# Second mixer of a two-layer encoder on one Trainium2 core: the fourth gated projection is written ahead of the attention

## The chip, the core and the metric

One core of a Trainium2 chip computes the whole network in one launch. Its engines are TensorE (PE, matrix products; PEld is its weight loading), VectorE (DVE), ScalarE (ACT, activation functions from tables that have to be loaded), GpSimd (POOL) and SyncE (SP, which issues DMAs). Each engine works through its own list of instructions in a fixed order; semaphores tie the lists together. The metric is the device time of one execution in microseconds (us), lower is better.

## The reference, cut to what matters

Two sequences of 256 tokens (512 tokens in all, width 1024, fp32) go through two layers. Layer 0 is another mixer and a feed-forward block; layer 1 is the mixer below and a feed-forward block of the same kind. The change touches only layer 1's mixer.

```
def odd_mixer(x, ...):
    h = x @ w_in
    c_q, c_kv, k_r, glu_a, glu_g = jnp.split(h, [o1, o2, o3, o4], axis=-1)
    c = latent_attention(c_q, c_kv, k_r, ...)          # 8 heads, softmax over 256 keys
    d = glu_a * jax.nn.sigmoid(glu_g)                  # 512 channels
    d = jax.nn.silu(layernorm(dwconv(d, conv_w, conv_b), conv_ln_g, conv_ln_b))   # 31 taps
    return jnp.concatenate([c, d], axis=-1) @ w_out
```

## The kernel before, in words

Every fp32 matrix product is split into three products of a rounded part and a remainder (`hi`, `lo`); `gemm_feat` issues them (recorded at L95, as all products). The layers run one after the other. A scheduler of the framework turns the written order into one list per engine; it moves instructions by its own estimate of when they can run, so the written order is a preference and not the final order.

In the second mixer the 512 gated channels are handled in four chunks of 128. For chunk i, `glu(i)` computes two products of 24 matrix instructions each, `glu` (value) and `glu` (gate), and calls `gate(i, ...)` at high priority: the sigmoid of the gate into `sig` (ACT, L551), the product into the padded tile `dpad` (DVE, L554), tap 0 of the convolution into `cacc` (DVE, L557), and tap 21 into `acc` (ACT, L559). The other 29 taps of a chunk are split: 20 run on DVE (L719, adding into `cacc`); for 9, ACT multiplies `dpad` by the tap into one of two slots of `pr` (L723) and POOL adds the slot to `acc` (L724). So an ACT product waits until POOL's add of two products earlier is done. L725 joins `cacc` and `acc`; `conv_ln` transposes the result (`ct`, L735), normalizes it and applies SiLU.

`attend(p)` does one pair of heads: per sequence and head a score set `s` (PE), the row maximum `nmx` (DVE, L491), the exponential into `er` with its sum (ACT, L494), the reciprocal `ri` (DVE, L497), the scaling of `er` (ACT, L501; DVE for the last pair), four transposes `pt` (PE, L508), a copy to `PTr` (ACT, L510), and per sequence the product `pv`, which is split into `mixT` (ACT L115, DVE L116). That makes 16 score sets. Only two score banks exist, so the scores of set n+2 wait for the exponential of set n.

Sigmoid and exponential stand in different ACT tables; a switch is an ACT_TABLE_LOAD. `preload(func, src)` runs a one-element activation into `tab` so that a load happens there. After the attention comes the output projection (`op`, `dn` tiles), whose weights and products also fill PE between the attention's last steps, and then the second feed-forward block, matrix products back to back.

Of the kernel before, what the change touches and what calls it, by code (L numbers as in the profile page):

```python
# [49 lines left out]
def tile_encoder(ctx: ExitStack, tc: tile.TileContext, I, O):  # L50
# [17 lines left out]
    def act(shape, dt=F32, s="a"):  # L68
        return actp.tile(shape, dt, tag="act", name=nm(s))

    def tmp(shape, dt=F32, s="t"):
        return tp.tile(shape, dt, tag="tmp", name=nm(s))
# [16 lines left out]
    def bank(pool, s="ps"):  # L89
        return pool.tile([P, 512], F32, tag="b", name=nm(s))  # L90
# [3 lines left out]
    def mm(out, lhsT, rhs, first, last):  # L94
        last_mm[0] = nc.tensor.matmul(out=out, lhsT=lhsT, rhs=rhs, start=first, stop=last)  # L95
# [6 lines left out]
    def preload(func, src):  # L102
        nc.scalar.activation(out=small(1, "tab"), in_=src, func=func)
# [27 lines left out]
    def pc(name, i):  # L131
        o, _ = PCOL[name]
        return par[:, o + i:o + i + 1]

    def gemm_feat(ps, hi, lo, xT, seqs=(0, 1), n=KC):
        if len(seqs) == 2:
            tsl = slice(0, T)
        else:
            tsl = slice(seqs[0] * S, seqs[0] * S + S)
        for k in range(n):  # L140
            xh, xl = xT[k][:, 0, tsl], xT[k][:, 1, tsl]
            wh, wl = hi[:, k * P:(k + 1) * P], lo[:, k * P:(k + 1) * P]
            mm(ps[:, tsl], wh, xh, k == 0, False)
            mm(ps[:, tsl], wh, xl, False, False)
            mm(ps[:, tsl], wl, xh, False, k == n - 1)
# [383 lines left out]
    def glu_load(i, keep=False):  # L529
        return [wload(I["wglu"][:, i, j].rearrange("p k n -> p (k n)"), 1024, keep) for j in range(2)]  # L530

    def odd_mixer(xT):
# [3 lines left out]
        def glu(i, by_seq=False):  # L536
            pss = []
            for hi, lo in kept.pop(i, None) or glu_load(i):
                pss.append((bank(pA, "glu"), hi, lo))
            for seqs in ((0,), (1,)) if by_seq else ((0, 1),):  # L540
                for ps, hi, lo in pss:
                    gemm_feat(ps, hi, lo, xT, seqs)
            with tc.high_priority():
                gate(i, pss[0][0], pss[1][0])

        def gate(i, pa, pg):
            sg = tmp([P, 512], s="sig")
            d = dpad[i]
            out, va = d[:, :, 15:15 + S], pa.rearrange("p (s t) -> p s t", s=2)
            vs = sg.rearrange("p (s t) -> p s t", s=2)  # L550
            nc.scalar.activation(out=sg, in_=pg, func=AF.Sigmoid)  # L551
            if i >= 2:
                preload(AF.Exp, sg[:, 0:1])
            nc.vector.tensor_tensor(out=out, in0=va, in1=vs, op=ALU.mult)  # L554
            accps[i] = bank(pA, "cacc")
            a, a2 = accps[i].rearrange("p (s t) -> p s t", s=2), acc2[i // 2][:, i % 2]
            nc.vector.tensor_scalar(out=a, in0=d[:, :, 0:S], scalar1=pc("cw", i * 32),  # L557
                                    scalar2=pc("cw", i * 32 + 31), op0=ALU.mult, op1=ALU.add)
            nc.scalar.activation(out=a2, in_=d[:, :, 31 - NPOOL:31 - NPOOL + S], func=AF.Copy,  # L559
                                 scale=pc("cw", i * 32 + 31 - NPOOL))  # L560
# [76 lines left out]
        def qproj():  # L637
            cT = G["cT"]
            wq = G["wq"]
            ropeT = G["kr"][:, 1:2, 0:S].broadcast_to([P, 2, S])  # L640
            qT = G["qT"] = [act([P, 2, T], s="qT") for _ in range(4)]

            def qfeat(pool, c):
                ps = bank(pool, "q")
                for k in range(2):
                    wh, wl = wq[k][0][:, c * P:(c + 1) * P], wq[k][1][:, c * P:(c + 1) * P]
                    mm(ps, wh, cT[k][:, 0, :], k == 0, False)
                    mm(ps, wh, cT[k][:, 1, :], False, False)
                    mm(ps, wl, cT[k][:, 0, :], False, k == 1)
                return ps  # L650
            for p in range(4):
                ps = qfeat(pB, 4 + p)
                for h in (0, 1):
                    rows = slice(64 - 64 * h, 128 - 64 * h)
                    nc.vector.tensor_tensor(out=qT[p][rows, h, :].rearrange("p (s t) -> p s t", s=2),  # L655
                                            in0=ps[rows].rearrange("p (s t) -> p s t", s=2), in1=ropeT[rows],
                                            op=ALU.mult)
                ps = qfeat(pC, p)
                for h in (0, 1):
                    rows = slice(64 * h, 64 * h + 64)  # L660
                    nc.scalar.activation(out=qT[p][rows, h, :], in_=ps[rows], func=AF.Copy, scale=96 ** -0.5)
# [20 lines left out]
        def attend(p):  # L682
            if p == 0:
                G["ring"] = Ring(2, "er"), Ring(2, "PTr")
            er, PTr = G["ring"]
            qT, kT = G["qT"][p], G["kT"][p]

            def score(out, qs, ks):
                for h in range(2):
                    mm(out[h], qT[:, h, qs], kT[:, h, ks], True, True)  # L690
            mixT[p] = act([P, 2, T], F32R, "mixT")
            if p == 2:
                G["sink"] = ToFeat(xscr[1], 1, last_mm[0], "ln1_g1", "ln1_b1", xscr[2], ())
            attention(p, score, G["V"], mixT[p], lambda ps, h, e: ps, er, PTr, p < 3, p == 3)
# [7 lines left out]
        kvproj()  # L702
        qproj()
        glu(2)
        attend(0)
        attend(1)
        glu(3)
        op = OutProj("wout1", mixT, [0, 1, 2, 3], [4, 5, 6, 7])
        attend(2)
        op.open(0)  # L710
# [126 lines left out]
    xT = even_mixer()  # L837
    xT = ffn(0, xT, lambda m: ToFeat(xscr[0], 0, m, "ln2_g0", "ln2_b0", xscr[1])).xT
    xT = odd_mixer(xT)
    ffn(1, xT, lambda m: ToOut(xscr[2], 2, m, 3, O["y"]))  # L840

# [80 lines left out]
```

## Time and profile before

| | before |
|---|---|
| time, median of 3 runs (lowest to highest) | 1106.43 us (1104.14 to 1106.67) |
| the profiled execution: its own time | 1104.76 us |
| the profiled execution: span from first to last instruction | 1102.9 us |
| PE busy in the span | 1082.3 us |
| granted TensorE clock, mean over the span | 0.992 |
| window 641.30 to 647.50 us: PE busy | 0.00 us |
| window 680.00 to 780.00 us: PE busy | 99.98 us |

The profile is of one execution, whose own time is 1.86 us longer than its span and 1.67 us shorter than the median of the three timed runs. All times in the trace are counted from the start of the span. PE is nearly always busy; the rows of the places where it is not are what has to be read.

### The profile page before, as it was taken

How to read it: one execution, taken by the hardware profiler on the slowest of the kernel's cores; microseconds unless marked ns; L12 is line 12 of the kernel's file. 1: busy time of each engine (PE TensorE's matmuls, PEld its weight loads, DVE VectorE, ACT ScalarE, POOL GpSimd, SP SyncE). 2: the span in 40 equal slices, each digit the busy share in tenths (PEclk: the TensorE clock that was granted, in tenths of full speed). 3: DMA queues.
4: the chain of work that ended last, by engine and by line, in shares of the span. 5: the costliest groups of instructions: out<-in, count | busy, mean ns of one | idle time of the engine just before them, and what ended most of it. 6: DMA issues, size and time to landing. Idle time of an engine off the chain costs nothing.

```text
span 1102.9 us, 13655 instructions
## 1 busy us (share of the span) xinstructions
PE 1082.3 (98%) x5210; PEld 900.8 (82%) x5210; DVE 673.2 (61%) x996; ACT 488.7 (44%) x783; POOL 226.6 (21%) x222
## 2 busy tenths in 40 slices
PE   9999999999999999999999979999999999999996
PEld 7888778988888888888898856899888888888885
DVE  5378955766565656422578999587665656542227
ACT  5436644544444444421266797355444444431110
POOL 0482001200000000005464661830000000000173
PEclk9999999999999999999999979999999999999999
DMA  7852223533333323645232104254333333222602
GB/s 256 244 141 77 60 103 107 163 105 96 96 96 96 96 96 99 206 166 180 80 122 58 38 20 153 66 172 122 100 96 96 96 96 96 96 96 96 215 34 76
DMA packets 36098, 124.21 MB, mean 113 GB/s; under 512 B 4289, under 2 KB 5057, under 8 KB 36033
## 3 DMA queue, kind: packets, MB, share of 16 engines
q1 hardware_dynamic: 28864, 100.05, 29.5%
q0 software_dynamic: 6448, 22.53, 6.0%
q8 instruction: 41, 0.67, 0.3%
q10 hardware_dynamic: 720, 0.75, 0.2%
q14 instruction: 25, 0.20, 0.1%
HBM read 113.88 MB, written 8.39 MB: 111 GB/s over the span
## 4 chain that ended last, share of the span: by engine, by line
PE 93%; DVE 3%; ACT 2%; issue 1%; DMA 0%; POOL 0%; POOLq 0%; DVEq 0%; ACTq 0%
PE up L95 44%; PE dn L95 29%; PE qk L95 4%; PE op L95 4%; PE glu L95 3%; PE v L95 2%; PE u L95 2%; PE s L95 1%; PE pv L95 1%; PE pt L508 1%; DVE cacc L719 1%; PE lnT L237 1%; DVE wlo L111 1%; DVE qT L655 0%; ACT er L494 0%
## 5 line engine op out<-in xcount | busy, mean ns | idle before, releaser
L95 PE MATMUL up<-xT,whi 128*128 128x512 f32 (+1 forms) x1536 | 439.9, 371 | 0.0
L111 DVE TENSOR_TENSOR wlo<-raw,whi 128x1024 fp32r<-128x1024 f32 (+1 forms) x174 | 238.8, 1374 | 297.4 <-ACT whi L109 296.1
L95 PEld LDWEIGHTS up<-xT,whi 128*128 128x128 f32 x1536 | 279.9, 188 | 49.9
L109 ACT CAST whi<-raw 128x1024 fp32r<-128x1024 f32 (+1 forms) x174 | 182.4, 1050 | 249.1 <-PE dn L95 132.6
L95 PE MATMUL up<-xT,wlo 128*128 128x512 f32 (+1 forms) x768 | 284.0, 372 | 0.0
L95 PE MATMUL dn<-whi,gT 128*128 128x512 f32 x704 | 217.4, 389 | 0.0
L95 PEld LDWEIGHTS up<-xT,wlo 128*128 128x128 f32 x768 | 144.4, 188 | 24.9
L95 PEld LDWEIGHTS dn<-whi,gT 128*128 128x128 f32 x704 | 132.0, 188 | 27.2
L95 PE MATMUL dn<-wlo,gT 128*128 128x512 f32 x352 | 136.9, 389 | 0.0
L186 POOL DMA_DIRECT2D xres<-xscr x12 | 6.5, 546 | 576.0 <-PE dn L95 576.0
L95 PEld LDWEIGHTS dn<-wlo,gT 128*128 128x128 f32 x352 | 66.1, 188 | 13.8
L115 ACT CAST gT<-cv 128x512 fp32r<-128x512 f32 x44 | 27.3, 620 | 111.6 <-DVE cv L782 111.6
L771 ACT ACTIVATE cv<-up,par 128x512 f32<-128x512 f32 x88 | 68.3, 776 | 0.0
L774 DVE SCALAR_TENSOR_TENSOR cv<-up,par,cv 128x510 f32<-128x510 f32 x88 | 65.8, 748 | 2.7
L781 ACT ACTIVATE cv<-cv 128x512 f32<-128x512 f32 x44 | 27.8, 632 | 85.2 <-DVE cv L774 85.2
L772 DVE SCALAR_TENSOR_TENSOR cv<-up,par,cv 128x510 f32<-128x510 f32 x88 | 65.4, 743 | 0.0
L719 DVE SCALAR_TENSOR_TENSOR cacc<-dpad,par,cacc 128x512 f32<-128x512 f32 x80 | 58.9, 750 | 1.1
L724 POOL TENSOR_TENSOR acc<-acc,pr 128x512 f32<-128x512 f32 x36 | 48.7, 1353 | 38.9 <-ACT pr L723 32.2
L116 DVE TENSOR_TENSOR gT<-cv,gT 128x512 fp32r<-128x512 f32 x44 | 30.4, 692 | 27.5 <-ACT gT L115 27.5
L95 PE MATMUL op<-whi,mixT 128*128 128x512 f32 x128 | 44.3, 402 | 0.0
L95 PE MATMUL dn<-whi,mixT 128*128 128x512 f32 x128 | 42.8, 394 | 0.0
L95 PE MATMUL glu<-xT,khi 128*128 128x512 f32 (+1 forms) x160 | 42.0, 349 | 0.0
(195 smaller groups left out, 1351.4 us busy)
## 6 DMA issues: line engine op xcount, KB each, us to landing
raw<-in_wup SPq DMA_DIRECT2D x88, 512.0 KB, 3.6
raw<-in_wdn SPq DMA_DIRECT2D x44, 512.0 KB, 3.5
raw<-in_wout SPq DMA_DIRECT2D x16, 512.0 KB, 3.7
xscr<-xres POOLq DMA_DIRECT2D x12, 512.0 KB, 3.7
xres<-xscr POOLq DMA_DIRECT2D x12, 512.0 KB, 4.4
raw<-in_wqk SPq DMA_DIRECT2D x8, 512.0 KB, 6.6
raw<-in_wglu SPq DMA_DIRECT2D x8, 512.0 KB, 3.8
raw<-in_wug SPq DMA_DIRECT2D x7, 512.0 KB, 3.6
```

Source lines behind the costliest of these rows:

```text
L95: last_mm[0] = nc.tensor.matmul(out=out, lhsT=lhsT, rhs=rhs, start=first, stop=last)
L109: nc.scalar.copy(out=hi[:, :n], in_=raw[:, :n])
L111: nc.vector.tensor_tensor(out=lo[:, :n], in0=raw[:, :n], in1=hi[:, :n].bitcast(F32), op=ALU.subtract)
L115: nc.scalar.copy(out=dst[:, 0, sl], in_=src)
L116: nc.vector.tensor_tensor(out=dst[:, 1, sl], in0=src, in1=dst[:, 0, sl].bitcast(F32), op=ALU.subtract)
L237: nc.tensor.transpose(self.banks[k // 2][:, (k % 2) * S + q * P:(k % 2) * S + q * P + P], x[:, k * P:(k + 1) * P], ident)
L719: nc.vector.scalar_tensor_tensor(out=a, in0=dpad[i][:, :, j:j + S], scalar=pc("cw", i * 32 + j), in1=a, op0=ALU.mult, op1=ALU.add)
L724: nc.gpsimd.tensor_tensor(out=a2, in0=a2, in1=pr, op=ALU.add)
L771: nc.scalar.activation(out=c, in_=pv, func=AF.Identity, scale=pc(fw, ch * 4 + 1), bias=pc(fw, ch * 4 + 3))
L772: nc.vector.scalar_tensor_tensor(out=c[:, :, 1:S], in0=pv[:, :, 0:S - 1], scalar=pc(fw, ch * 4), in1=c[:, :, 1:S], op0=ALU.mult, op1=ALU.add)
L774: nc.vector.scalar_tensor_tensor(out=c[:, :, 0:S - 1], in0=pv[:, :, 1:S], scalar=pc(fw, ch * 4 + 2), in1=c[:, :, 0:S - 1], op0=ALU.mult, o ...
L781: nc.scalar.activation(out=cg, in_=cg, func=AF.Silu)
```

## The change

`glu(3)` is written ahead of `attend(0)` and `attend(1)` in place of behind them, and the load of the exponential's table is asked for once, behind the fourth sigmoid, in place of behind the third and again behind the fourth.

```
             nc.scalar.activation(out=sg, in_=pg, func=AF.Sigmoid)
-            if i >= 2:
+            if i == 3:
                 preload(AF.Exp, sg[:, 0:1])
             nc.vector.tensor_tensor(out=out, in0=va, in1=vs, op=ALU.mult)
...
         kvproj()
         qproj()
         glu(2)
+        glu(3)
         attend(0)
         attend(1)
-        glu(3)
         op = OutProj("wout1", mixT, [0, 1, 2, 3], [4, 5, 6, 7])
```

Since a scheduler sets the lists, the lists themselves show what moves. On ACT, before, this stands from the scaling of the first score set to the exponential of the third (`er_5018` is first used by score sets 0 and 1, `er_5019` by 2 and 3; `sig_5243` is the fourth gate):

```order
L501 ACTIVATE er_5018<-er_5018,ri_5038 128x256 x2
L723 ACTIVATE pr_4428<-dpad_4418,par 128x512
L494 ACTIVATE er_5018,rs_5050<-s_5028,nmx_5048 128x256 x2
L501 ACTIVATE er_5018<-er_5018,ri_5053 128x256 x2
L551 ACT_TABLE_LOAD
L551 ACTIVATE sig_5243<-glu_5194 128x512
L510 COPY PTr_5022<-pt_5042 128x512
L559 ACTIVATE acc_705_4425<-dpad_4421,par 128x512
L723 ACTIVATE pr_4428<-dpad_4421,par 128x512 x2
L494 ACT_TABLE_LOAD
L494 ACTIVATE er_5019,rs_5071<-s_5063,nmx_5069 128x256 x2
```

In the changed kernel ACT has this from the last products of the third chunk to the exponential of the second score set (`sig_5066` is the fourth gate, `er_5074` serves score sets 0 and 1):

```order
L723 ACTIVATE pr_4428<-dpad_4418,par 128x512 x6
L551 ACTIVATE sig_5066<-glu_5017 128x512
L103 ACT_TABLE_LOAD
L103 ACTIVATE tab_5068<-sig_5066 128x1
L559 ACTIVATE acc_705_4425<-dpad_4421,par 128x512
L723 ACTIVATE pr_4428<-dpad_4421,par 128x512 x2
L494 ACTIVATE er_5074,rs_5091<-s_5083,nmx_5089 128x256 x2
L723 ACTIVATE pr_4428<-dpad_4421,par 128x512 x2
L501 ACTIVATE er_5074<-er_5074,ri_5094 128x256 x2
L494 ACTIVATE er_5074,rs_5106<-s_5084,nmx_5104 128x256 x2
```

The two exponentials that stood ahead of the fourth sigmoid now stand behind it, all nine products of the third chunk stand ahead of it, and one table load is left where there were two (a third, behind the third sigmoid `sig_5010`, is gone as well).

On PE, before, the first two score sets stand among the products of the fourth chunk (`glu_5193` value, `glu_5194` gate):

```order
L95 MATMUL glu_5193<-xT_4287,khi_3989 128x512 x2
L95 MATMUL s_5027<-kT_4684,qT_4884 128x256 x2
L95 MATMUL glu_5193<-xT_4287,klo_3991 128x512
L95 MATMUL glu_5194<-xT_4252,khi_3995 128x512 x2
L95 MATMUL glu_5194<-xT_4252,klo_3997 128x512
L95 MATMUL s_5028<-kT_4684,qT_4884 128x256 x2
```

In the changed kernel the 48 products come first and the score sets behind them:

```order
L95 MATMUL glu_5017<-xT_4287,khi_3995 128x512 x2
L95 MATMUL glu_5017<-xT_4287,klo_3997 128x512
L95 MATMUL s_5083<-kT_4684,qT_4884 128x256
L95 MATMUL s_5084<-kT_4684,qT_4884 128x256
L95 MATMUL s_5083<-kT_4684,qT_4884 128x256
L95 MATMUL s_5084<-kT_4684,qT_4884 128x256
L95 MATMUL s_5119<-kT_4684,qT_4884 128x256 x2
L508 MATMUL pt_5098<-ident,er_5074 128x128 x4
```

So the first scores start after the fourth chunk has left PE, and the third score set is the first thing behind them that has to wait for an exponential.

Further on PE, before, the part around the fifth score set's transposes (`pt_5122`) reads as follows (`op` is the output projection, `mixT_5026` the first pair's result):

```order
L95 MATMUL s_5150<-kT_4685,qT_4885 128x256 x2
L95 MATMUL op_916_5457<-whi_5353,mixT_5026 128x512
L95 MATMUL op_916_5457<-wlo_5355,mixT_5026 128x512
L95 MATMUL op_917_5458<-whi_5353,mixT_5026 128x512
L95 MATMUL op_917_5458<-wlo_5355,mixT_5026 128x512
L508 MATMUL pt_5122<-ident,er_5018 128x128 x4
```

In the changed kernel three transposes of the convolution's sums (`ct_5641`, from `acc_704` for chunks 0 and 1 and `acc_705` for chunk 2) stand ahead of the fifth set's transposes (`pt_5178`):

```order
L95 MATMUL s_5206<-kT_4685,qT_4885 128x256 x2
L95 MATMUL op_915_5455<-whi_5351,mixT_5082 128x512
L95 MATMUL op_915_5455<-wlo_5353,mixT_5082 128x512
L95 MATMUL op_916_5456<-whi_5351,mixT_5082 128x512
L95 MATMUL op_916_5456<-wlo_5353,mixT_5082 128x512
L735 MATMUL ct_5641<-ident,acc_704_4424 128x128 x2
L735 MATMUL ct_5641<-ident,acc_705_4425 128x128
L508 MATMUL pt_5178<-ident,er_5074 128x128 x4
```

Before, those three transposes stood behind the scores of the ninth set. Past the first few column blocks of the second feed-forward block the lists of all engines are the same as before but for buffer numbers, and SP's list of DMAs is the same throughout.

## Rows read from the trace of the kernel before

**Rows 1.** The page: busy time, share of span, instructions; chain of waits by engine.
```profile
PE 1082.3 (98%) x5210; PEld 900.8 (82%) x5210; DVE 673.2 (61%) x996; ACT 488.7 (44%) x783; POOL 226.6 (21%) x222
...
PE 93%; DVE 3%; ACT 2%; issue 1%; DMA 0%; POOL 0%; POOLq 0%; DVEq 0%; ACTq 0%
```

**Rows 2.** Windows: length, busy by engine (instructions), granted clock, DMA share, GB/s.
```profile
644.00:645.00 1.00, 0.00 (x0) 0.00 (x0) 1.00 (x2) 1.00 (x2) 0.42 (x1) 0.69 0.00 0
644.40:658.00 13.60, 9.48 (x27) 5.53 (x28) 13.19 (x24) 13.57 (x33) 9.56 (x8) 0.50 0.01 2
658.00:680.00 22.00, 20.42 (x120) 14.48 (x119) 20.85 (x44) 20.55 (x63) 5.60 (x9) 1.00 0.46 167
680.00:780.00 100.00, 99.98 (x578) 85.95 (x577) 71.37 (x124) 48.94 (x81) 34.81 (x27) 1.00 0.36 111
```

**Rows 3.** Timeline of PE: start, duration, operation, count, idle before and its releaser.
```profile
625.87 0.62 PE L95 MATMUL glu<-xT,khi 128*128 128x512 f32 x2
...
626.55 0.62 PE L95 MATMUL glu<-xT,khi 128*128 128x512 f32 x2
...
638.54 1.02 PE L95 MATMUL s<-kT,qT 128*128 128x256 f32 x4
...
647.50 2.07 PE L95 MATMUL s<-kT,qT 128*128 128x256 f32 x4 [6.20 <-ACT er L494]
...
659.29 0.60 PE L508 MATMUL pt<-ident,er 128*128 128x128 f32 x4
```

**Rows 4.** Timeline of ACT, from the third sigmoid to the last product.
```profile
621.99 0.60 ACT L551 ACTIVATE sig<-glu 128x512 f32<-128x512 f32 x1 [0.16 <-PE glu L95]
622.61 1.28 ACT L103 ACT_TABLE_LOAD   x1
...
625.86 1.18 ACT L661 ACTIVATE qT<-q 64x512 f32<-64x512 f32 x2
...
634.64 0.73 ACT L723 ACTIVATE pr<-dpad,par 128x512 f32<-128x512 f32 x1 [1.50 <-POOL acc L724]
635.40 0.48 ACT L494 ACTIVATE er<-s,nmx 128x256 f32<-128x256 f32 x1
...
636.31 0.72 ACT L723 ACTIVATE pr<-dpad,par 128x512 f32<-128x512 f32 x1
636.93 0.90 ACT L501 ACTIVATE er<-er,ri 128x256 f32<-128x256 f32 x2
637.73 0.72 ACT L723 ACTIVATE pr<-dpad,par 128x512 f32<-128x512 f32 x1
...
640.51 1.28 ACT L551 ACT_TABLE_LOAD   x1
641.81 0.60 ACT L551 ACTIVATE sig<-glu 128x512 f32<-128x512 f32 x1
642.30 0.58 ACT L510 COPY PTr<-pt 128x512 f32<-128x512 f32 x1
643.17 0.72 ACT L559 ACTIVATE acc<-dpad,par 128x512 f32<-128x512 f32 x1 [0.28 <-DVE dpad L554]
...
645.13 1.28 ACT L494 ACT_TABLE_LOAD   x1
646.43 0.47 ACT L494 ACTIVATE er<-s,nmx 128x256 f32<-128x256 f32 x1
...
665.51 0.23 ACT L103 ACTIVATE tab<-sig 128x1 f32<-128x1 f32 x1
```

**Rows 5.** Timeline of POOL: the first two adds of the third chunk.
```profile
625.41 2.67 POOL L724 TENSOR_TENSOR acc<-acc,pr 128x512 f32<-128x512 f32 x2 [7.40 <-ACT pr L723]
```

**Rows 6.** Windows of ACT alone: length, busy (instructions), clock, DMA share, GB/s.
```profile
646.43:677.19 30.76, 29.90 (x84) 0.81 0.33 120
```

**Rows 7.** Timeline of DVE: the fourth gate's product and the third chunk's sum.
```profile
642.44 0.69 DVE L554 TENSOR_TENSOR dpad<-glu,sig 128x512 f32<-128x512 f32 x1 [1.41 <-ACT sig L551]
...
660.34 0.69 DVE L725 TENSOR_TENSOR acc<-cacc,acc 128x512 f32<-128x512 f32 x1
```

More of the change, by code (lines that the diff above doesn't have):

```diff
@@ L551, in gate @@
             nc.scalar.activation(out=sg, in_=pg, func=AF.Sigmoid)
-            if i >= 2:
+            if i == 3:
                 preload(AF.Exp, sg[:, 0:1])
@@ L704, in odd_mixer @@
         glu(2)
+        glu(3)
         attend(0)
         attend(1)
-        glu(3)
         op = OutProj("wout1", mixT, [0, 1, 2, 3], [4, 5, 6, 7])
```

## The prediction

> **What bounds the kernel now.** The page comes first: PE is busy for 1082.3 of 1102.9 us and is 93% of the chain that ended last [rows 1]. A change can only pay where PE waits or where its clock is low, so I looked for those places in windows. From 680 us on PE is busy for 99.98 of 100 us [rows 2]: whatever the mixer gains before 680 us moves all that follows, and nothing behind it can hide or add much. Just before lies the worst place of the run. PE stands idle for 6.20 us up to 647.50, waiting for an exponential `er` on ACT [rows 3]. During that wait its granted clock falls (mean 0.69 in 644 to 645), and it stays at 0.50, the 1.2 GHz level, from 644.40 to 658.00 [rows 2]. From there to 680 it is back at 2.4 GHz and busy for 20.42 of 22.00 us.
>
> The timeline of ACT says why PE waits [rows 4]. The first score set's exponential starts at 635.40, but behind the second set ACT loads the sigmoid's table at 640.51, makes the fourth gate at 641.81, waits 0.28 for the gate's product on DVE, computes tap 21 and two tap products, and loads the exponential's table again at 645.13; the third exponential starts at 646.43, and it frees the bank that PE waits for. The reader should not stop at PE's 6.2 us, though. From that exponential to 677.19 ACT is busy for 29.90 of 30.76 us [rows 6], and in the 13.60 us of low clock for 13.57 [rows 2]. ACT sets the pace of the attention. What PE gains in the end is what ACT's queue gains.
>
> **The change part by part.** *Removed.* Two of the three table loads between 622 and 646 us go, 1.28 us each, and one of the two one-element activations, 0.23: 2.79 us of ACT [rows 4]. The wait of 0.28 for the gate's product goes too, since the one load that is left lies between the sigmoid and tap 21 and covers DVE's 0.69 [rows 4, 7]. That is 3.07 us, if nothing takes its place.
>
> Here a page can be weighed against rows. Each load starts at the end of the instruction before it and the next one starts 0.02 us after its 1.28 (640.51, then 641.81) [rows 4], so a load is 1.28 us here and no more. The Trainium skill (ScalarE: Activation LUTs, section "What ACT_TABLE_LOAD costs") gives 1283 ns for the load, which agrees, and adds about 1380 ns of drain, 2.66 us per switch; the trace shows no room for the drain. By the page two loads would be worth 5.3 us in place of the rows' 2.56.
>
> *Moved.* The fourth chunk's 48 products start at 625.87 and go at three in 0.68 us (625.87 to 626.55) [rows 3], so 16 times 0.68, 10.9 us: with no scores among them they end at about 636.9 in place of 638.54. But the sigmoid now stands behind all nine tap products of the third chunk as well. These are paced by POOL, whose undisturbed adds take 1.33 us each (2.67 for two) [rows 5]; ACT waited 1.50 for a slot before the seventh product, which started at 634.64, the eighth at 636.31 and the ninth at 637.73 [rows 4]. Of the first load's 1.28 I count 0.4 as won there, since tap 21 then waits for DVE's product of 0.69 instead: the seventh at 634.2, the ninth two adds later at 636.9, ending 0.62 later (636.31 to 636.93) at 637.5. So products and slots let the sigmoid go at about 637.5, 4.3 us earlier than now.
>
> What is late next: the exponentials, all queued behind that sigmoid. From the third sigmoid's start to the end of two tap products ACT needs 621.99 to 625.86, 3.87 us, with a load in it [rows 4]; the same sequence behind the fourth puts the first exponential at 641.4, against 635.40 now, and ACT has nothing to do in the slots between POOL's adds, which two exponentials and their scalings filled before. PE meets this at the third score set: scores 1 and 2 end at about 637.8, the first exponential (0.91, from 635.40 to 636.31 [rows 4]) frees the bank at 642.3, so PE idles for some 4.5 us in place of 6.2. The wait is moved and shortened, not removed.
>
> Now ACT's position. In the new order there stand from the first exponential to the third: exponential 0.91; two products, 0.62 each, with some 0.5 of waiting for POOL (two adds last 2.67, so the slot of the second comes free late); scaling 0.80 (636.93 to 637.73); exponential 0.91; product 0.62; copy 0.5 (0.58 with its end overlapped); product 0.62; scaling 0.80 [rows 4, 5]. That is 6.9 us: the third exponential starts at 641.4 + 6.9 = 648.3, which is 1.9 later than 646.43. But by then six of the fourth chunk's nine products are done where two were done before; four more at 0.62 are 2.5 us of ACT's work. ACT is ahead by 2.5 - 1.9 = 0.6 us.
>
> *Sum.* From there ACT has the same instructions left in both kernels but for the 0.23 at 665.51, and little waiting to lose [rows 6], so PE leaves the attention about 0.6 us earlier: 1104.76, the profiled execution's own time, less 0.6 is 1104.2. That execution is 1.67 below the median of the runs shown, whose lowest is 1104.14; I give the changed kernel's median as **1105.0**, half of that distance back. Against the median it is a gain of 0.1%, and about 0.3%, 3.3 us, is what a measurement of this kernel can tell from no change.
>
> *What costs nothing.* The two one-element memory settings and the buffer numbers that move cost nothing visible under a busy DVE. The earlier fourth chunk lets DVE start chunk four's taps some 4 us earlier and saves its wait of 1.41 us at 642.44 [rows 7], but the attention waits for ACT, so this is cover: it would count only if DVE were the later one. No DMA moves, since SP's list is the same. In the output projection PE's order differs, with no wait that I can see, as the weights it needs are converted as early as before; the cover is PE's own queue, busy for 99.98 of 100 us.
>
> *Bounds.* The new idle on ACT between 622 and 637 is not shown by any row. Were it nothing, the whole 3.07 would come back; were the sigmoid 0.6 later than 637.5 (POOL's adds slower by 0.1 each would do it), nothing would. Every further us there costs one. I take 0.6 because it follows POOL's pace, the nearest row.
>
> **The rivals.** *The removed work comes back whole.* ACT is busy for nearly all of the attention, which speaks for it; POOL's pace, which leaves ACT idle ahead of the sigmoid, against. It gives 1104.76 - 3.07 = 1101.7.
>
> *The gap shrinks enough to keep the clock.* In this trace the clock fell once inside a gap of 6.2 us; the 1.58 us of idling spread over 658 to 680 did not lower it [rows 2, 3]. One of 4.5 may or may not. If it does not fall, and if PE were the later engine there, PE would get back half of the 9.48 us that it worked at 0.50 [rows 2], 4.7, and 1.7 of the gap: 1104.76 - 6.4 = 1098.4. The Trainium skill (TensorE: Matmul & The Clock Gate, section "HAM oscillation — how this bites in real kernels") makes idle gaps between bursts of products the cause of such a fall, and the trace agrees as far as its one fall goes. Against the price stands ACT, busy for 13.57 of these 13.60 us: a PE at full clock would wait for it instead.
>
> *The new order of PE makes a wait (slower).* Three transposes `ct` now stand ahead of the fifth score set's `pt`. They need DVE's sum of the third chunk, which ended at 660.34 + 0.69 = 661.03, while the fifth set's `pt` started at 659.29 [rows 3, 7]. If DVE gains nothing, PE, arriving 0.6 earlier, waits 661.03 - 658.7 = 2.3 us, all of it passed on to ACT through the `PTr` copy: 2.3 - 0.6 = 1.7 slower, 1106.5. It decides from a wait of 0.6 on. Against it: DVE loses its wait of 1.41, which alone brings the sum to 659.6, and the sum stands one score set earlier in DVE's list.
>
> That the change does nothing is excluded for ACT's list, in which the loads are gone.
>
> **How the numbers follow.** The forecast (2 us faster to 1 us slower than 1104.76) has 0.62, the loads coming back whole 0.14, the kept clock 0.10, the new wait 0.14. Faster by over 0.3%: the kept clock's 0.10, half of the whole return 0.07, and 0.03 from the forecast's edge: 0.20. Slower by over 0.3%: 0.04, since even the full wait is 1.7 us. Same: 0.76. The range goes from 1101.0, just under the whole return, to 1108.2, the new wait's 1106.5 with the 1.67 by which the median can stand above a profiled run; that leaves out the kept clock and little else. The forecast alone reaches from 1102.8 to 1107.4.
>
> **What would show it right or wrong.** In the changed kernel's profile: one load behind the fourth sigmoid, which starts between 637 and 638; ACT waiting for POOL several times before it; the first exponential near 641.4; a PE gap of 4 to 5 us ending near 642; the third exponential near 648; ACT over 95% busy from there to 677; PE without gaps past 680. I am wrong if the sigmoid goes before 636, if PE's gap is under 3 us, if PE's `ct` waits over 1 us near 658, or if PE, not ACT, is waited for in the stretch between 650 and 675.

## The result, and the profile after

The changed kernel is slower, by 0.8%. It takes 1113.36 us (median of 4 runs, 1112.63 to 1114.46) against 1105.29 for the kernel before beside it (4 runs, 1104.05 to 1106.67): a ratio of 1.0081, 95% interval [1.0069, 1.0093]. I had forecast 1105.0 and a range up to 1108.2. The profiled execution took 1112.63 us (span 1110.9), 7.87 more than the one before.

The stretch that the prediction was made for went as it said. The timeline of ACT in the changed kernel, around the fourth sigmoid, answers to [rows 4]:

```profile
636.97 0.72 ACT L723 ACTIVATE pr<-dpad,par 128x512 f32<-128x512 f32 x1 [0.63 <-POOL acc L724]
637.72 0.60 ACT L551 ACTIVATE sig<-glu 128x512 f32<-128x512 f32 x1
638.33 1.28 ACT L103 ACT_TABLE_LOAD   x1
...
641.58 0.45 ACT L494 ACTIVATE er<-s,nmx 128x256 f32<-128x256 f32 x1
...
648.61 0.47 ACT L494 ACTIVATE er<-s,nmx 128x256 f32<-128x256 f32 x1
...
660.99 0.58 ACT L510 COPY PTr<-pt 128x512 f32<-128x512 f32 x1 [0.84 <-PE pt L508]
```

The sigmoid starts at 637.72 behind a wait for POOL, one load follows, the first exponential starts at 641.58 and the third at 648.61; 637.5, 641.4 and 648.3 were forecast. The loss lies behind 680 us. Windows of the changed kernel (length, busy by engine, granted clock, DMA share, GB/s) answer to [rows 2]:

```profile
644.00:645.00 1.00, 0.74 (x3) 0.04 (x1) 1.00 (x3) 1.00 (x3) 1.00 (x1) 0.50 0.00 0
680.00:700.00 20.00, 16.08 (x87) 11.37 (x86) 17.92 (x30) 8.17 (x22) 15.70 (x8) 0.88 0.09 26
700.00:720.00 20.00, 20.00 (x91) 16.13 (x88) 9.14 (x9) 7.49 (x11) 6.24 (x3) 0.95 0.27 79
720.00:820.00 100.00, 100.00 (x550) 87.22 (x549) 66.39 (x109) 48.15 (x70) 11.44 (x16) 1.00 0.39 121
```

PE was busy throughout the 100 us behind 680 before [rows 2]; now it stands idle for 3.92 us between 680 and 700, and its clock drops to the 1.2 GHz level for part of 680 to 720. Behind 720 PE is busy throughout at full clock again, as before. PE's timeline in the changed kernel, answering to [rows 3], says who is waited for:

```profile
642.63 2.08 PE L95 MATMUL s<-kT,qT 128*128 128x256 f32 x4 [4.08 <-ACT er L494]
...
691.38 0.55 PE L508 MATMUL pt<-ident,er 128*128 128x128 f32 x3 [0.81 <-DVE er L503]
...
693.84 0.30 PE L508 MATMUL pt<-ident,er 128*128 128x128 f32 x1 [0.97 <-DVE er L503]
696.10 0.90 PE L508 MATMUL pt<-ident,er 128*128 128x128 f32 x3 [1.96 <-DVE er L503]
696.93 3.68 PE L95 MATMUL pv<-PTr,V 128*64 128x256 f32 x16
700.54 0.80 PE L95 MATMUL op<-whi,mixT 128*128 128x512 f32 x1
```

The last transposes of the attention wait for L503, the scaling of `er` on DVE. So DVE's timeline there, in the changed kernel, and POOL's at the same time:

```profile
685.34 1.22 DVE L111 TENSOR_TENSOR wlo<-raw,whi 128x1024 fp32r<-128x1024 f32 x1
...
687.07 4.25 DVE L503 TENSOR_SCALAR er<-er,ri 128x256 f32<-128x256 f32 x2
...
692.36 3.68 DVE L503 TENSOR_SCALAR er<-er,ri 128x256 f32<-128x256 f32 x2
```

```profile
684.85 0.55 POOL L166 TENSOR_TENSOR rstd<-rstd,epsc 128x1 f32<-128x1 f32 x1 [2.08 <-DVE ri L497]
685.36 10.53 POOL L194 TENSOR_TENSOR xres<-xres,rowg 128x1024 f32<-128x1024 f32 x4
695.86 10.38 POOL L197 TENSOR_TENSOR xres<-xres,rowb 128x1024 f32<-128x1024 f32 x4
```

The first four of these POOL instructions and the four scalings one by one, in the changed kernel:

```profile
685.36 3.43 POOL L194 TENSOR_TENSOR xres<-xres,rowg 128x1024 f32<-128x1024 f32 x1
688.75 2.42 POOL L194 TENSOR_TENSOR xres<-xres,rowg 128x1024 f32<-128x1024 f32 x1
691.14 2.41 POOL L194 TENSOR_TENSOR xres<-xres,rowg 128x1024 f32<-128x1024 f32 x1
693.50 2.39 POOL L194 TENSOR_TENSOR xres<-xres,rowg 128x1024 f32<-128x1024 f32 x1
```

```profile
687.07 1.87 DVE L503 TENSOR_SCALAR er<-er,ri 128x256 f32<-128x256 f32 x1
688.86 2.46 DVE L503 TENSOR_SCALAR er<-er,ri 128x256 f32<-128x256 f32 x1
692.36 1.33 DVE L503 TENSOR_SCALAR er<-er,ri 128x256 f32<-128x256 f32 x1
693.62 2.43 DVE L503 TENSOR_SCALAR er<-er,ri 128x256 f32<-128x256 f32 x1
```

The same instructions in the kernel before, DVE (with two weight remainders `wlo`) and POOL:

```profile
683.26 1.22 DVE L111 TENSOR_TENSOR wlo<-raw,whi 128x1024 fp32r<-128x1024 f32 x1
...
686.33 0.59 DVE L503 TENSOR_SCALAR er<-er,ri 128x256 f32<-128x256 f32 x2
...
689.12 0.59 DVE L503 TENSOR_SCALAR er<-er,ri 128x256 f32<-128x256 f32 x2
...
693.48 2.68 DVE L111 TENSOR_TENSOR wlo<-raw,whi 128x1024 fp32r<-128x1024 f32 x1 [0.94 <-PE pv L95]
```

```profile
689.85 0.55 POOL L166 TENSOR_TENSOR rstd<-rstd,epsc 128x1 f32<-128x1 f32 x1 [2.24 <-DVE rstd L165]
690.36 10.41 POOL L194 TENSOR_TENSOR xres<-xres,rowg 128x1024 f32<-128x1024 f32 x4
```

Read together: two scalings take 0.59 us before and 4.25 and 3.68 now. What lies over them is POOL's work on the residual tiles `xres`, eight instructions of 128x1024 that `affine` issues behind the last `rstd` of the convolution's normalization. With the fourth chunk early, that `rstd` comes 5.00 us earlier (684.85 against 689.85), POOL starts at 685.36 in place of 690.36, and the last four scalings, which were done at 689.71 before, now fall under it. They go in step with POOL: each of the four scalings ends 0.15 us (to about 0.01) behind the end of one of POOL's four `xres` instructions, the first at 688.94 behind 688.79. PE waits 3.91 us (0.81, 0.17 for `cnm`, 0.97, 1.96), its clock falls, and it works 6.10 of the 6.80 us from 695.4 to 702.2 at a granted 0.51, which by this clock costs some 3 us more (an estimate, half of 6.10). Together that is 6.9 of the 7.87 us. This is the theory; the rival is that the attention's own delay and clock made the loss.

The kernel before shows such a wait already, and I had overlooked it: a `wlo` of 1.22 us takes 2.68 at 693.48, under POOL's work that starts at 690.36. There PE doesn't wait for it, so nothing on PE's timeline pointed to it.

### The profile page after: what moved, and what is told of

Its sections match the earlier page's. It is cut to its first block, busy times and chain, and to the rows that moved or that the text cites. A ratio compares the mean times of both kernels' runs of the same rounds, so it can differ in the third digit from the quotient of the medians.

```text
span 1110.9 us, 13644 instructions
## 1 busy us (share of the span) xinstructions
PE 1087.3 (98%) x5210; PEld 902.2 (81%) x5210; DVE 676.0 (61%) x996; ACT 485.9 (44%) x780; POOL 225.1 (20%) x222
## 4 chain that ended last, share of the span: by engine, by line
PE 91%; DVE 3%; ACT 2%; POOL 1%; issue 1%; DMA 0%; POOLq 0%; DVEq 0%; ACTq 0%
PE up L95 43%; PE dn L95 28%; PE qk L95 4%; PE op L95 4%; PE glu L95 3%; PE v L95 2%; PE u L95 2%; PE pv L95 1%; PE s L95 1%; PE pt L508 1%; PE lnT L237 1%; DVE er L503 1%; POOL acc L724 1%; ACT pr L723 1%; ACT er L494 0%
## 5 line engine op out<-in xcount | busy, mean ns | idle before, releaser
L111 DVE TENSOR_TENSOR wlo<-raw,whi 128x1024 fp32r<-128x1024 f32 (+1 forms) x174 | 234.8, 1351 | 290.3 <-ACT whi L109 288.0
```

What stands on the lines that cost most here:

```text
L111: nc.vector.tensor_tensor(out=lo[:, :n], in0=raw[:, :n], in1=hi[:, :n].bitcast(F32), op=ALU.subtract)
```

## The experiments

**e1: POOL's residual work later.** In the changed kernel the multiplications wait for the attention's last product.

```
         flush_pv()
+        last_pv = last_mm[0]
...
                     with tc.issue_after(last_pow[0].ins):
-                        sink.res.affine(range(NT))
+                        sink.res.affine(range(NT), last_pv)
```

> The changed kernel, with one edit: POOL's eight multiplications and additions on the residual tiles xres (128x1024 each) wait for the last product pv of the attention. Nothing is left out. Theory (collision): in the changed kernel these start at 685.36 us, 5.00 earlier than before (690.36), and lie over the last four scalings of er on DVE, which take 2.02 us each there and 0.34 before; with them out of the way the scalings take 0.3 to 0.4 us again, PE waits less than 0.5 us for any of them, the output projection's first product op moves from 700.5 to about 693 to 694, and the time is 1104 to 1107. Rival (the attention itself: exponentials later by 1.0 to 1.6 us, the lower clock, the transposes ct ahead of the fifth set): the time stays at 1110 or more, since none of these is touched. Between 1107 and 1110 both have a part.

1105.07 us, ratio to before 1.0004 [0.9995, 1.0013]. In e1, the scalings (count, then least/median/most duration in ns, first and last start) and PE's first `op`:

```profile
L503 DVE TENSOR_SCALAR er<-er,ri x4: 341/344/345, 687.1 to 689.3; 128x256 f32<-128x256 f32 x4
```

```profile
693.71 0.50 PE L95 MATMUL op<-whi,mixT 128*128 128x512 f32 x1
```

The same scalings, started at the same 687.1, take 0.34 us, and `op` starts at 693.71 in place of 700.54. PE's list is that of the changed kernel, the attention's waits and clock up to 680 are too (PE's gap is 4.06 us against 4.08, the clock 0.66 over 640 to 660 in both), and all 8 us are back. The rival falls.

**e2: another form of the scaling.** `tensor_tensor` with `ri` broadcast in place of `tensor_scalar`, for the last pair.

```
+                    elif last_pair:
+                        nc.vector.tensor_tensor(out=e[:, qt, :], in0=e[:, qt, :],
+                                                in1=ri[:, qt:qt + 1].broadcast_to([P, 256]), op=ALU.mult)
```

> The changed kernel, with the scalings of the last pair of heads on DVE written as a product of two tensors (er and ri broadcast over 256 columns) in place of a tensor and a scalar. POOL's residual work starts as early as in the changed kernel. If DVE is held off only in the form with one tensor in SBUF and a scalar: the new form takes 0.4 to 0.8 us under POOL's work, most of the 8 us come back, 1105 to 1108. If any DVE instruction that reads and writes SBUF waits for POOL's current instruction: 1.5 to 2.5 us each as now, 1110 to 1114. If the collision is not the cause, the time stays at 1112 to 1114 whatever the duration is.

1112.42 us, 1.0078 [1.0061, 1.0095]. First the line in the changed kernel, then in e2:

```profile
L503 DVE TENSOR_SCALAR er<-er,ri x4: 1331/2146/2464, 687.1 to 693.6; 128x256 f32<-128x256 f32 x4
```

```profile
L503 DVE TENSOR_TENSOR er<-er,ri x4: 1135/2359/2596, 687.7 to 693.7; 128x256 f32<-128x256 f32 x4
```

The form makes no difference: with two tensors read, a scaling is held as long.

**e3: POOL's residual work in pieces.** Each instruction cut into four of 256 columns, started as early as in the changed kernel.

```
+                for r, op in ((0, ALU.mult), (1, ALU.add)):
+                    for c in range(0, D, D // cut):
+                        sl = slice(c, c + D // cut)
+                        nc.gpsimd.tensor_tensor(out=x[:, sl], in0=x[:, sl], in1=self.rows[r][:, sl], op=op)
...
-                        sink.res.affine(range(NT))
+                        sink.res.affine(range(NT), 4)
```

> The changed kernel, with POOL's residual work of this mixer cut into pieces of 256 columns (32 instructions in place of 8, the same arithmetic, started as early). If a scaling on DVE waits until the POOL instruction of that moment has ended: a piece is about 0.65 to 0.9 us, so a scaling takes 0.4 to 1.2 us, mean about 0.8, PE waits some 2 us in place of 3.7, and the time is 1105 to 1109. If DVE is slowed for as long as POOL is busy: about 2 us each as now, 1111 to 1115. Rival (the attention itself): no change, 1112 to 1114.

1105.05 us, 1.0005 [0.9996, 1.0014]. The scalings in e3, under POOL's pieces (mean 0.88 us):

```profile
L503 DVE TENSOR_SCALAR er<-er,ri x4: 340/610/823, 687.2 to 689.6; 128x256 f32<-128x256 f32 x4
```

POOL is busy over the same stretch without a gap, as in the changed kernel, yet a scaling waits at most 0.48 us. So what it waits for is the end of POOL's instruction, not of POOL's work; with some 0.3 us more for each, PE does not wait for them. e11 below limits that reading.

**e4: one instruction early in the kernel before.**

```
-                if t == NT - 1:
+                if t >= NT - 2:
                     with tc.issue_after(last_pow[0].ins):
-                        sink.res.affine(range(NT))
+                        if t == NT - 2:
+                            sink.res.affine((0,), rows=(0,))
+                        else:
+                            sink.res.affine((0,), rows=(1,))
+                            sink.res.affine((1, 2, 3))
```

(`affine` is also given a parameter `rows`, which picks the multiplication or the addition.)

> The kernel before, with one of POOL's eight residual instructions (the first multiplication, 128x1024) put ahead of the fourth rstd, behind the third: it then starts at about 687.6 us in place of 690.4 and lies over the scaling that starts at 689.12. Order on PE differs a little from the kernel before (a product pv and a block of cb change places). Theory (collision): one scaling of that pair of two goes from 0.34 to between 1.2 and 2.2 us and ends with POOL's instruction, the other stays near 0.35, the fourth rstd comes 0.3 to 1.2 us later, and the kernel gets 1 to 2 us slower than before. Rival: the scalings keep 0.34 us, and the time is that of before within 0.5 us.

1104.48 us, 1.0000 [0.9990, 1.0009]. In e4, the scaling pair (from 688.36) and POOL's instruction:

```profile
L503 DVE TENSOR_SCALAR er<-er,ri x2: 341/668/994, 688.4 to 689.3; 128x256 f32<-128x256 f32 x2
```

```profile
686.82 2.39 POOL L195 TENSOR_TENSOR xres<-xres,rowg 128x1024 f32<-128x1024 f32 x1
```

One scaling is held to POOL's end at 689.21, ends 0.15 us behind it and takes 0.99, the other 0.34. That is the theory's pattern, though a shorter wait than the 1.2 to 2.2 expected: a wait of 0.65 us does not show in the time, and my 1 to 2 us were wrong.

**e5: the table loads put back**, in the kernel of e3, where no collision hides their price.

```
-            if i == 3:
+            if i >= 2:
```

> The kernel of the pieces (fourth projection early, residual work of 256 columns a piece, 1105.05 us) with the two table loads put back: the exponential's table is asked for behind the third sigmoid too, so the sigmoid's is loaded again ahead of the fourth. Only ACT gets two loads (1.28 us each) and a one-element activation (0.23) more. This measures what the removed loads are worth, free of the collision. My prediction's account (3.07 us of ACT taken away, waiting for POOL's slots eats a part): the first load lies in ACT's wait for POOL and costs nothing, the second delays the fourth sigmoid and all exponentials behind it, so the sigmoid starts near 639.0 in place of 637.7, the third exponential near 649.9 in place of 648.6, and the time is 1105.5 to 1107.5. Rival (ACT has slack behind 650, or DVE sets the pace): the time stays within 0.5 us of 1105.05.

1107.0 us, 1.0019 [1.0011, 1.0028]. ACT in e5, from the third sigmoid on, and that sigmoid in the changed kernel:

```profile
622.55 0.60 ACT L551 ACTIVATE sig<-glu 128x512 f32<-128x512 f32 x1 [0.16 <-PE glu L95]
...
637.99 0.72 ACT L723 ACTIVATE pr<-dpad,par 128x512 f32<-128x512 f32 x1 [0.64 <-POOL acc L724]
638.73 1.28 ACT L551 ACT_TABLE_LOAD   x1
640.02 0.60 ACT L551 ACTIVATE sig<-glu 128x512 f32<-128x512 f32 x1
...
650.92 0.46 ACT L494 ACTIVATE er<-s,nmx 128x256 f32<-128x256 f32 x1
```

```profile
621.90 0.60 ACT L551 ACTIVATE sig<-glu 128x512 f32<-128x512 f32 x1 [0.17 <-PE glu L95]
```

The profiled execution of e5 is 0.65 us later already at the third sigmoid, ahead of both loads. Counted from there, the third exponential comes 1.66 us later than in the changed kernel, and the time is 1.5 (by the ratios) to 1.95 us longer than e3's. The second load moves the sigmoid by its 1.28; the first, which I had taken as free, moves the last product ahead of it by 0.37 and no more, near the 0.4 of the prediction. So the order alone costs about 2 us against before, and the loads that it saves give about that back.

**e6: scaling from PSUM.** The last two heads' second sequence keeps its exponentials in the score banks.

```
-                    nc.scalar.activation(out=e[:, qt, :], in_=sc[:, qt, :], func=AF.Exp,
+                    nc.scalar.activation(out=(sc if last_pair and s else e)[:, qt, :], in_=sc[:, qt, :], func=AF.Exp,
...
-                        nc.vector.tensor_scalar(out=e[:, qt, :], in0=e[:, qt, :], scalar1=ri[:, qt:qt + 1],
+                        nc.vector.tensor_scalar(out=e[:, qt, :], in0=(sc if last_pair and s else e)[:, qt, :],
```

> The changed kernel with the exponentials of the last two heads' second sequence left in their score banks in PSUM; DVE scales them from there into er. Nothing is left out; some of the products dn that fill PE come later than in the changed kernel, since they wait for these banks. POOL's residual work is as early as in the changed kernel. If only DVE instructions whose tensors all lie in SBUF are held off by POOL: these scalings take 0.35 to 0.5 us under POOL's work (the copies PTr from PSUM kept 0.68 there), and the time is 1104 to 1107. If any instruction that writes SBUF can be held: 1.5 to 2.5 us each, 1110 to 1114.

1107.27 us, 1.0023 [1.0014, 1.0032], just above the 1104 to 1107 that was expected: 6 us of the 8 are back. The held banks also change PE's order, and what the other 2 us are is not shown. Scalings in e6, and POOL over them:

```profile
L503 DVE TENSOR_SCALAR er<-s,ri x4: 471/471/472, 688.8 to 691.7; 128x256 f32<-128x256 f32 x4
```

```profile
687.09 10.49 POOL L194 TENSOR_TENSOR xres<-xres,rowg 128x1024 f32<-128x1024 f32 x4
```

Read from PSUM, four scalings take 0.47 us each, to within 1 ns, under the same POOL instructions, though they write to SBUF. So it takes the source in SBUF too for a scaling to be held. No run shows this form without POOL beside it; that it isn't held is read from the four equal times.

**e7, e12 and e14: an order that keeps a gain.** Both gated projections ahead of the queries' projection, with POOL's residual work in pieces (e7), whole and early (e12), and whole behind the last `pv` as in e1 (e14).

```
-        qproj()
         glu(2)
         glu(3)
+        qproj()
```

> The kernel of the pieces, with the third and the fourth gated projection written ahead of the projection of the queries in place of behind it. Nothing is left out. If what is left of the loss in the attention is ACT's empty time ahead of the fourth sigmoid (4.3 us of waits for POOL's slots): the sigmoid goes some us earlier, ACT fills its waits with the copies of the queries, PE's gap at 642 shrinks below 2 us, and the time is 1100 to 1104. If POOL's 36 additions or DVE's taps set the end: 1104 to 1107, no gain.

> The order of e7 (third and fourth gated projection ahead of the projection of the queries) with POOL's residual work in whole instructions of 1024 columns. It tells how much of e7's time rests on the pieces. If the convolution ends as early as in the changed kernel, the residual work starts near 685 and meets the last scalings again: 2 us a scaling, 1110 to 1114. If it ends late enough or the scalings come earlier than that work: 1103 to 1105, as e7.

> The order of e7 (third and fourth gated projection ahead of the projection of the queries) with POOL's residual work whole, and behind the last pv as in e1: the candidate that should meet neither the scalings (0.34 us each) nor, being whole, hold a DVE instruction for more than one of its own. If the collision is all that e12 lost (1111.04): 1103 to 1104.5, as e7 in pieces (1103.69). If the weights' remainders on DVE behind 693 now meet the residual work at a worse place: above 1105.

e7 takes 1103.69 us, 0.9990 [0.9982, 0.9999]; e12 1111.04, 1.0060 [1.0047, 1.0073]; e14 1103.62, 0.9990 [0.9982, 0.9999]. The scalings in e12, and in e14:

```profile
L503 DVE TENSOR_SCALAR er<-er,ri x4: 1321/2145/2465, 685.4 to 692.0; 128x256 f32<-128x256 f32 x4
```

```profile
L503 DVE TENSOR_SCALAR er<-er,ri x4: 342/346/348, 685.4 to 687.6; 128x256 f32<-128x256 f32 x4
```

With another order ahead of it the collision has the same size, and the same cure: e12 and e14 differ by that one dependency alone, and by over 7 us. e14 and e7 are level and the fastest here, 0.1% below before. That e7 lies in the range expected for it does not confirm its reason: PE's gap was to shrink below 2 us, and it is 3.92 us in e7 and 3.93 in e14. What gives the 0.1% is not shown.

**e8 to e11: pieces in the kernel before.** The cut of e3, put into the kernel before and nothing else.

> The kernel before, with the same cut of POOL's residual work into pieces of 256 columns and nothing else. A control: in the kernel before no scaling lies under that work. Theory: within 0.5 us of the kernel before, so that the 7 us which the pieces give back to the changed kernel are the collision's. Rival (smaller pieces are a gain by themselves, wherever they stand): 3 us or more faster than before.

> The same kernel as the control e8, whose twelve times fell in two groups (six of 1103.9 to 1104.7, six of 1113.3 to 1115.1), looked at again for the place of the second group; its profile was of the first. If this execution takes 1113 us or more: (a) the collision at another place: a DVE instruction with its tensors in SBUF lies long under a POOL piece ahead of 700 us and PE waits for it by some us; (b) POOL's pieces end late (715.7 in the first group) and DVE's residual sums and so PE wait behind 715; (c) the granted clock falls for some 19 us where it did not in the first group, without a new wait. If it takes 1104 us it tells nothing new.

> The control e8 once more, timed on another chip. If its two groups belong to the kernel (POOL's pieces finer than before meet something at a varying moment), some of its executions take 1113 us or more here too, and the profile, if it is of one of these, shows the place: (a) ahead of 700 us, (b) behind 715 us, or (c) the clock alone. If all take 1104 to 1105.5 us, the second group was of that one call, and the control holds: the pieces give the kernel before nothing and cost it nothing.

The control turned into a finding. e8's ratio of 1.0040 [1.0014, 1.0065] is a mean over two groups of times: 6 of 1103.93 to 1104.74, 6 of 1113.33 to 1115.1. e9 (1104.04) and e10 (1105.15), one execution each, were of the first. e11, on another chip, had 5 of 10 in each (1103.96 to 1104.35, 1113.39 to 1116.08; ratio 1.0035 [1.0007, 1.0063]), and its profile is of the second. It is the only profile of that group. The same weight remainder on DVE in e8's profile, which is of the first group, then DVE, POOL and PE in e11:

```profile
702.75 1.39 DVE L111 TENSOR_TENSOR wlo<-raw,whi 128x1024 fp32r<-128x1024 f32 x1 [7.10 <-ACT whi L109]
```

```profile
703.66 10.98 DVE L111 TENSOR_TENSOR wlo<-raw,whi 128x1024 fp32r<-128x1024 f32 x1 [7.08 <-ACT whi L109]
```

```profile
701.16 8.32 POOL L197 TENSOR_TENSOR xres<-xres,rowb 128x256 f32<-128x256 f32 x12
709.43 1.40 POOL L197 TENSOR_TENSOR xres<-xres,rowg 128x256 f32<-128x256 f32 x2
710.79 2.76 POOL L197 TENSOR_TENSOR xres<-xres,rowb 128x256 f32<-128x256 f32 x4
```

```profile
714.69 0.80 PE L95 MATMUL dn<-wlo,mixT 128*128 128x512 f32 x1 [7.37 <-DVE wlo L111]
```

This single instruction, which took 1.39 us in e8's profile, is held in e11 until POOL's last piece ends (710.79 + 2.76 = 713.55) and ends 1.09 us later. It is the same collision, at a place that I had not named, in a kernel whose list on PE is that of before; PE waits 7.37 us for it, and its clock falls (0.74 over 700 to 720, against 1.00 in e8). So pieces are no safe cure: an instruction that doesn't get in between two of them can be held by the whole row. The 10 times of e3 lay within 1.7 us and the 11 of e7 within 0.8, so neither showed a second group.

**e13: the transposes `ct` back behind the ninth set's scores**, in the kernel of e1.

```
+                if p == 2:
+                    G.setdefault("s9", last_mm[0])
...
+                    with tc.issue_after(G["s9"].ins):
+                        nc.tensor.transpose(ps[:, c * P:(c + 1) * P],
...
```

> The kernel of e1 (residual work behind the last pv) with the convolution's first three transposes ct put back behind the ninth set's scores, where they stand in the kernel before; nothing else moves. It tests the forecast's slower rival at its place, and where the 0.6 us that I forecast went. If these transposes ahead of the fifth set's pt cost (ACT waits 0.84 us for that pt in the changed kernel, and they take 0.33 us there): the wait falls to about 0.5 and the time is 0.3 to 1.0 us below e1's 1105.07. If they only fill time: within 0.3 us of e1.

1104.99 us, 1.0005 [0.9996, 1.0014]: level with e1. ACT's wait for the fifth set's `pt` falls to 0.52 us, as expected, but the time does not follow: these transposes cost the kernel nothing that can be measured.

## Why the prediction was wrong

**Right: the front half.** That the sigmoid follows POOL's slots, that the exponentials move behind it, and that PE's wait shrinks from 6.20 to 4.5 (4.08 measured) without going away all held. The loss does not come from there.

**The step that failed** is in the first paragraph: whatever comes before 680 moves all that follows, "and nothing behind it can hide or add much", with its companion under what costs nothing, that the earlier fourth chunk on DVE "is cover". PE had no gap behind 680, so I looked for no other engine there. But the fourth chunk's taps also end the convolution; its last `rstd` frees eight POOL instructions, and they start 5.00 us earlier, onto DVE's last scalings. I had asked what the moved step changes for DMAs and for PE, and not for POOL's queue. e1 shows the cause by taking the overlap away: 8 us, all of the loss. Of the signs that I had named, "PE without gaps past 680" is the one that gave it away.

**Mis-sized: the 0.6 us.** The loads are worth 1.5 to 2 us (e5) where my sum had 3.07 less POOL's waits, but the order around them costs as much, so that without the collision the change is level (1.0004 and 1.0005), `op` being 0.40 us later than before in e1's profile and not 0.6 earlier. That e1's 1105.07 lies beside the 1105.0 that I had forecast is no confirmation, since the kernel before takes 1104.46 beside it. The term at fault is "little waiting to lose". The stretch of [rows 6] ends where the thirteenth set's exponential starts; that exponential starts at 678.78 in the changed kernel. From the third exponential to it ACT is idle for 2.50 of 30.17 us, against 0.86 of 30.76 before, 0.84 of it for the fifth set's `pt`; the sign "ACT over 95% busy" failed with 92%. The window of ACT alone, in the changed kernel:

```profile
648.61:678.78 30.17, 27.67 (x81) 0.91 0.34 115
```

What makes these waits stays open. The `ct` transposes are behind 0.32 us of them, and e13 shows that this moves no time. ACT did not set the pace to the end, either: that exponential is 1.59 us later than before, and `op` in e1 0.40.

**The rivals.** The slower one named the wrong place: the third chunk's sum ends at 658.25 in the changed kernel and the `ct` start at 660.02, with no wait. The clock was not kept: in 644 to 645 it is 0.50, behind a gap of 4.08 us. The whole return did not come.

## What to carry to other kernels

When a step is moved earlier, follow what its end releases on every queue, down to work that nobody is waiting for, and ask what runs on the engine beside it at the new time. An elementwise job on POOL that is not urgent is best tied to the end of the stage whose DVE work is urgent, as in e14, and not to its own inputs alone. A repair that merely makes the overlap finer has to be timed many times before it is trusted. And where an instruction takes longer than others of its shape (2.68 against 1.22 us here, in the kernel before), ask what ran beside it, even where nothing waits for it yet.

## What the runs showed of the hardware

In these runs DVE and POOL hold each other off where both read from SBUF and write to it. A DVE scaling of 128x256 takes 0.34 us alone and 1.33 to 2.46 beside POOL instructions of 128x1024 (2.39 each), and ends 0.15 us behind the end of one of them; with its source in PSUM it took 0.47 beside the same work (e6). It works in the other direction too: while DVE's 1.22 us `wlo` ran from 685.34, POOL's first `xres`, started at 685.36, took 3.43 in place of 2.39.

The Trainium skill (GPSIMD Engine Reference, section "Key points") says that GpSimd shares its SBUF interfaces with VectorE, in contention with DVE instructions in a two-port mode or with two SBUF inputs; e2, with two SBUF inputs, agrees with it, and so does e6, whose source is not in SBUF. Whether the plain scaling runs in a two-port mode no trace here shows. That section gives no price. Here the price was up to the rest of the POOL instruction that was running (2.12 us, 2.46 less 0.34), and in e11 9.89 us of a row of pieces for one DVE instruction. Why a waiting DVE instruction gets in between two pieces in some executions and not in others stays open.
